# Moving the S5 gate's matrix products behind two more projection tiles in the hand-written order of a hybrid trunk's mixing stage

## The chip, the core and the metric

The kernel runs on one core of one Trainium2 chip. The metric is the device time of one execution in microseconds (us), lower is better. The kernel before takes 1447.62 us in the median of three runs.

## The reference, cut to what matters

The model has two layers. Each layer is a half-step SwiGLU feed-forward block, a mixing block and a second half-step feed-forward block, on 272 tokens (16 learned ones and 256 of the input) of width 1024. The mixing block projects once and feeds four head groups of width 512:

```python
proj = h @ w_in                       # 1024 -> 5136, split into the groups' inputs
y_a = rglru_mixer(a_x, a_gate, ...)   # group A
y_b = gdn_mixer(b_qkv, ...)           # group B: a triangular solve in chunks
y_c = ssd_mixer(c_z, c_xbc, ...)      # group C
y_d = s5_mixer(d_u, ...)              # group D
y = concatenate([y_a, y_b, y_c, y_d]) @ w_out
```

The change is about the end of group D. After its state-space scan has given `y` (512 channels), the S5 mixer does

```python
y = y.reshape(bsz, t, W_GRP) + d_skip * uf
y = jax.nn.gelu(y)
y = y * jax.nn.sigmoid(y @ w_glu.astype(F32))   # the S5 gate: a 512 x 512 product
return rms_norm(y, norm_g)
```

## The kernel before

**Products.** Channels lie on the 128 partitions and tokens along the free dimension. Every large product is made in three passes (`mm3`, lines 229 to 234): the weight and the activation are each split into a rounded part and a remainder, and hi*xh, hi*xl and lo*xh are added up in one PSUM tile. A weight tile is 128 x 1024 (512 KB). It is loaded by SyncE into one of three `raw` buffers (`load`, line 205), split by ScalarE into `hi` (line 215) and by VectorE into `lo` (line 217), four buffers each. `ahead(3)` (line 208) is called behind each tile and keeps three tiles split in advance. The order of the weights is read from the same list of steps that orders the work (`weights`, line 99), so moving a step moves its load and its split with it.

**PSUM.** The products of the weight tiles write into tiles named `g`, from a pool of four; everything smaller writes into `m`, from a second pool of four:

```python
s.pg = pool('pg', 4, bass.MemoryType.PSUM)
s.pm = pool('pm', 4, bass.MemoryType.PSUM)
...
def gps(s):
    return s.pg.tile([P, 512], F32, name=s.nm('g'), tag='g')
```

A `g` tile can be given out again once its last reader is done.

**The mixing stage** walks through `STEPS` (lines 81 to 88), a list written out by hand. A name with a number is one step. The names that this text needs:

- `du`, `k`, `q`, `v`, `cB`, `cC`, `cx`, `cz`, `ax`: one w_in tile each, that is 24 products of 272 (or 256) columns into one `g` tile (`one_tile`, line 323), and behind them the unit that reads this tile. For `q`, `k`, `v`, `cB`, `cC` and `cx` the unit is a four-tap convolution (`conv`, lines 538 to 545: one ScalarE instruction and three VectorE instructions on line 545, all four reading the `g` tile) and a SiLU (lines 551 and 552); for `ax` it is the convolution alone, into `s5b` (line 876; step `ax0` also loads two small weights, line 874); for `cz` the SiLU alone.
- `da0` to `da3`: the skip and the GELU of S5, one quarter of the channels each (lines 1229 and 862 to 865, ScalarE and VectorE in turn). `ds0` to `ds3`: the split of that quarter for `mm3`, into `dU` by ScalarE (line 1236) and `du` by GpSimd (line 1237).
- `dg0`, `dg1`: the S5 gate (`d_glu`, lines 1240 to 1254). Each is one tile of w_glu and fills two `g` tiles with 12 products each, tanh on ScalarE (line 1250) and a gating product on VectorE (line 1252) behind each of the two.
- `dn0`, `dn1`: S5's norm. `bm`, `bf`, `bs`, `bt`, `bo`: the triangular solve of group B (its products are on line 686). `bc`: the chain of small VectorE instructions ahead of that solve (lines 656 to 671), queued behind the last convolution unit before it in the list, `cB1`. `cg`: a product of group C on line 803. `bv2`: transposes on line 628.

```python
def d_glu(s, i):
    ...
    w = s.chunk()
    for m in (2 * i, 2 * i + 1):
        ps = s.gps()
        for k in range(4):
            s.mm3(ps[:, 0:s.N], w, (m % 2) * 4 + k, s.dyh[:, k], s.dyl[:, k], k == 0, k == 3)
```

**The order on each engine** is fixed when the program is built: the tile framework takes the instructions in the order in which the steps issue them as their priority and places them on a modelled timeline, so an instruction that is ready in the model can pass one that is not. Each engine then runs its own list strictly in order on the chip.

Of the kernel before, what the change touches and what calls it, by code (L numbers as in the profile page):

```python
# [80 lines left out]
STEPS_TEXT = '''  # L81
du0 du1 du2 du3 k0 di0 k1 sm k2 do0 tk ks1 R0 ks0 q0 q1 di1 q2 k3 cB0 do1 qs0 qs1 ks3 ks2 q3 di2 qs3 cz0 v0 v1 da0 qs2
do2 v2 be0 di3 bn cC0 bg0 R1 v3 be1 da1 do3 bg1 bg2 cx0 da2 bg3 bv0 da3 cC1 bb bv1 ds0 cB1 bc bm0 cz1 cx1 ds1 cg0 cg1 ds2
ds3 bv2 dg0 ax0 bf00 dg1 bm1 ax1 dn0 bf01 bf02 cx2 bf03 cx3 dn1 ax2 cz2 bf10 bf04 bs00 bf11 bs01 xd0 am2 am1 bs02 ax3
am0 xd1 bs03 am3 bs04 bf12 S0 bf13 ce0 bf14 ag0 bs10 bs11 cz3 bs12 ac ag1 bs13 bs14 bz0 S1 bz1 as0 ag2 xd2 bt0 bz2 ag3
as1 as2 bt1 as3 bz3 bo00 cp0 an0 ce1 S2 bo10 bo30 an1 ce2 bo31 bo01 bo20 cp1 oA0 bo11 bo21 S3 cp2 bo02 cn00 bo32 ce3
bo22 cn01 bo12 cp3 oB0 cn10 cn11 oD0 oC0 oD1 oB1 oA1 oC1
# [1427 lines left out]
```

## Time and profile before

| | before |
|---|---|
| median of three runs | 1447.62 us |
| lowest and highest run | 1442.08 and 1450.54 us |
| the profiled execution's own time | 1442.42 us |
| its span, first to last instruction | 1440.5 us |
| mean granted TensorE clock | 0.969 of 2.4 GHz |
| matmul busy (PE), weight load busy (PEld) | 1392.0 us, 1353.8 us |
| VectorE (DVE), ScalarE (ACT), GpSimd (POOL) busy | 1036.4, 708.4, 205.4 us |

A timeline row gives the start, the duration, the engine, the line, the operation, the output and its inputs by the names of tiles, the shapes, how many equal instructions were merged, and in square brackets the idle time before it with what ended that idle time. `g` and `m` are PSUM tiles, `r` a scratch tile, `xh` and `xl` the split activation.

### The profile page before, as it was taken

Reading aid. Unit: us, or ns where it says so; the run is one execution under the profiler, and the core shown is the slowest. Engines: PE = TensorE matmul, PEld = TensorE weight load, DVE = VectorE, ACT = ScalarE, POOL = GpSimd, SP = SyncE. Lnnn points to the kernel's source line nnn. Section 1 sums busy time; section 2 is a strip of 40 time slices with the busy share of each in tenths; the row PEclk is TensorE's granted clock in tenths of the full one; section 3 lists DMA queues with packets and bytes.
Section 4 is the critical chain, followed back from the end, with each engine's and each line's share of the span. In section 5 each row is a group of like instructions: output and inputs, shape, how many; then the busy total and the mean of one; then the engine's idle time right before and its main releaser. Section 6 shows DMA issues by size and latency. Waiting matters only on the chain. (4 is left out here: it accounts for less than half of the span.)

```text
span 1440.5 us, 27604 instructions
## 1 busy us (share of the span) xinstructions
PE 1392.0 (97%) x10848; PEld 1353.8 (94%) x10848; DVE 1036.4 (72%) x1936; ACT 708.4 (49%) x1226; POOL 205.4 (14%) x235
## 2 busy tenths in 40 slices
PE   7999999998999999999999999999989899999997
PEld 7999998997998999999999999989989889999997
DVE  6998787978985468887656665669888746666653
ACT  6445444454675355554444444444555745544442
POOL 1000010322322320000100000103332223100011
PEclk9999999999997999999999999999999979999998
DMA  7568775654422256777555555556544213666662
GB/s 238 179 188 265 235 254 163 217 171 120 126 77 71 82 155 217 254 230 254 172 162 184 175 170 174 172 161 211 177 127 141 74 45 114 186 187 187 188 182 85
DMA packets 94025, 243.73 MB, mean 169 GB/s; under 512 B 29496, under 2 KB 39496, under 8 KB 93896
## 3 DMA queue, kind: packets, MB, share of 16 engines
q1 hardware_dynamic: 93896, 241.97, 54.2%
q8 instruction: 85, 1.39, 0.4%
q14 instruction: 44, 0.36, 0.1%
HBM read 222.16 MB, written 19.78 MB: 168 GB/s over the span
## 5 line engine op out<-in xcount | busy, mean ns | idle before, releaser
L215 ACT ACTIVATE hi<-raw 128x1024 fp32r<-128x1024 f32 (+1 forms) x382 | 403.3, 1056 | 532.2 <-PE g L233 302.0
L217 DVE TENSOR_TENSOR lo<-raw,hi 128x1024 fp32r<-128x1024 f32 (+1 forms) x382 | 470.2, 1231 | 215.6 <-ACT hi L215 213.9
L232 PE MATMUL g<-xh,hi 128*128 128x272 f32 (+1 forms) x2048 | 597.7, 293 | 12.2 <-ACT hi L215 8.7
L234 PE MATMUL g<-xh,lo 128*128 128x272 f32 (+1 forms) x2048 | 595.8, 292 | 0.8 <-DVE lo L217 0.8
L233 PE MATMUL g<-xl,hi 128*128 128x272 f32 (+1 forms) x2048 | 595.3, 291 | 0.3 <-DVE xl L317 0.3
L232 PEld LDWEIGHTS g<-xh,hi 128*128 128x128 f32 x2048 | 391.4, 191 | 14.7 <-ACT hi L215 8.6
L234 PEld LDWEIGHTS g<-xh,lo 128*128 128x128 f32 x2048 | 390.7, 191 | 2.6 <-DVE lo L217 1.1
L233 PEld LDWEIGHTS g<-xl,hi 128*128 128x128 f32 x2048 | 391.5, 191 | 1.5 <-DVE xl L317 0.6
L277 POOL TENSOR_TENSOR acc<-acc,r 128x272 f32<-128x272 f32 (+1 forms) x42 | 43.3, 1032 | 556.1 <-ACT r L276 555.4
L233 PE MATMUL g<-r,hi 128*128 128x272 f32 (+1 forms) x256 | 73.2, 286 | 0.0
L360 DVE TENSOR_TENSOR r<-r,g 128x272 f32<-128x272 f32 (+1 forms) x88 | 38.1, 432 | 37.5 <-PE g L234 36.0
L545 DVE SCALAR_TENSOR_TENSOR r<-g,small,r 128x269 f32<-128x269 f32 (+2 forms) x120 | 59.1, 493 | 2.0 <-ACT r L542 0.4
L234 PE MATMUL g<-ra,lo 128*128 128x272 f32 (+1 forms) x192 | 55.2, 287 | 0.0
L232 PE MATMUL g<-ra,hi 128*128 128x272 f32 (+1 forms) x192 | 55.1, 287 | 0.0
L233 PE MATMUL g<-rs,hi 128*128 128x272 f32 (+1 forms) x192 | 55.0, 286 | 0.0
L233 PE MATMUL g<-rz,hi 128*128 128x272 f32 (+1 forms) x192 | 55.0, 286 | 0.0
L234 PE MATMUL g<-rq,lo 128*128 128x272 f32 (+1 forms) x192 | 54.6, 287 | 0.0
L232 PE MATMUL g<-rq,hi 128*128 128x272 f32 (+1 forms) x192 | 53.5, 289 | 0.2
L358 DVE TENSOR_TENSOR r<-g,rstd 128x272 f32<-128x272 f32 (+1 forms) x88 | 38.3, 435 | 15.6 <-PE g L234 14.8
L233 PEld LDWEIGHTS g<-r,hi 128*128 128x128 f32 x256 | 48.1, 188 | 0.0
L232 PE MATMUL g<-dU,hi 128*128 128x272 f32 (+1 forms) x96 | 29.7, 309 | 9.8 <-DVE r L545 9.8
L359 ACT ACTIVATE r<-r 128x272 f32<-128x272 f32 (+1 forms) x88 | 36.5, 415 | 5.4 <-DVE r L358 4.2
(412 smaller groups left out, 2461.5 us busy)
## 6 DMA issues: line engine op xcount, KB each, us to landing
raw<-in_wgu_dram SPq DMA_DIRECT2D x176, 512.0 KB
raw<-in_wdn_dram SPq DMA_DIRECT2D x88, 512.0 KB
raw<-in_win_dram SPq DMA_DIRECT2D x80, 512.0 KB
raw<-in_wout_dram SPq DMA_DIRECT2D x32, 512.0 KB
s5a<-spill SPq DMA_DIRECT2D x8, 920.0 KB
s5b<-spill SPq DMA_DIRECT2D x8, 896.0 KB
spill<-s5a SPq DMA_DIRECT2D x8, 648.0 KB
spill<-rx SPq DMA_DIRECT2D x4, 640.0 KB
```

What stands on the lines that cost most here:

```text
L215: nc.scalar.activation(out=hi[:, 0:w], in_=raw[:, 0:w], func=AF.Copy)
L217: ins = nc.vector.tensor_tensor(out=lo[:, 0:w], in0=raw[:, 0:w], in1=hi[:, 0:w].bitcast(F32), op=ALU.subtract)
L232: nc.tensor.matmul(ps, lhsT=hi, rhs=xh, start=start, stop=False)
L233: nc.tensor.matmul(ps, lhsT=hi, rhs=xl, start=False, stop=False)
L234: nc.tensor.matmul(ps, lhsT=lo, rhs=xh, start=False, stop=stop)
L277: (eng or nc.gpsimd).tensor_tensor(out=acc, in0=acc, in1=t, op=ALU.add)
L358: nc.vector.tensor_tensor(out=t, in0=g[:, t0], in1=r, op=ALU.mult)
L359: nc.scalar.activation(out=si, in_=t, func=AF.Silu)
L360: nc.vector.tensor_tensor(out=a, in0=si, in1=u[:, t0], op=ALU.mult)
L545: nc.vector.scalar_tensor_tensor(out=dst[:, o:T], in0=ps[:, 0:T - o], scalar=taps[:, j:j + 1], in1=dst[:, o:T], op0=ALU.mult, op1=ALU.add)
```

## The change

In the list of steps, both steps of the S5 gate and the first step of its norm move back, and the list is otherwise the same. `dg0` stood ahead of `ax0` and now stands behind `ax1`; `dg1` stood between `ax0` and `ax1` and now stands behind `cx2`; `dn0` now stands behind `cx3`.

```diff
-ds3 bv2 dg0 ax0 bf00 dg1 bm1 ax1 dn0 bf01 bf02 cx2 bf03 cx3 dn1 ax2 cz2 bf10 bf04 bs00 bf11 bs01 xd0 am2 am1 bs02 ax3
+ds3 bv2 ax0 bf00 ax1 dg0 bm1 cx2 dg1 bf01 bf02 cx3 dn0 bf03 ax2 dn1 cz2 bf10 bf04 bs00 bf11 bs01 xd0 am2 am1 bs02 ax3
```

The list serves both layers, so the change is made twice.

## Rows read from the trace of the kernel before

**Rows 1.** The page: span, and busy time by engine.
```profile
span 1440.5 us, 27604 instructions
...
PE 1392.0 (97%) x10848; PEld 1353.8 (94%) x10848; DVE 1036.4 (72%) x1936; ACT 708.4 (49%) x1226; POOL 205.4 (14%) x235
```

**Rows 2.** Waits of PE over the whole span: total us, times, longest us.
```profile
PE g L232 <- DVE r L545: 9.8, 2, 6.0
...
PE m L686 <- DVE E L816: 4.9, 1, 4.9
```

**Rows 3.** PE's timeline in the first layer, around the first gate products.
```profile
356.47 0.57 PE L232 MATMUL g<-dU,hi 128*128 128x272 f32 x1 [5.98 <-DVE r L545]
...
360.69 0.39 PE L232 MATMUL g<-dU,hi 128*128 128x272 f32 x1
...
361.55 0.62 PE L803 MATMUL m<-dc 128*128 128x272 f32 x2
...
362.85 0.37 PE L232 MATMUL g<-xh,hi 128*128 128x272 f32 x1
...
365.94 0.29 PE L232 MATMUL g<-dU,hi 128*128 128x272 f32 x1
```

**Rows 4.** PE's timeline in the second layer, the same place.
```profile
1070.63 0.36 PE L232 MATMUL g<-dU,hi 128*128 128x256 f32 x1 [3.87 <-DVE r L545]
...
1074.37 0.28 PE L234 MATMUL g<-dU,lo 128*128 128x256 f32 x1
```

**Rows 5.** One stretch by engine: busy us (instructions) of PE, PEld, DVE, ACT, POOL; granted clock; DMA.
```profile
350.00:360.00 10.00, 4.02 (x19) 3.83 (x19) 6.94 (x16) 5.26 (x12) 3.00 (x4) 0.70 0.41 139
```

**Rows 6.** GpSimd's timeline: the last split of the S5 quarters, both layers.
```profile
355.39 0.76 POOL L1237 TENSOR_TENSOR du<-dp,dU 128x272 fp32r<-128x272 f32 x1 [0.84 <-ACT dU L1236]
...
1069.53 0.72 POOL L1237 TENSOR_TENSOR du<-dp,dU 128x256 fp32r<-128x256 f32 x1 [0.81 <-ACT dU L1236]
```

**Rows 7.** VectorE's timeline in the first layer.
```profile
354.10 0.75 DVE L865 SCALAR_TENSOR_TENSOR dp<-r,r 128x272 f32<-128x272 f32 x1 [0.50 <-ACT r L864]
354.77 1.55 DVE L545 SCALAR_TENSOR_TENSOR r<-g,small,r 128x269 f32<-128x269 f32 x3
356.88 0.44 DVE L552 SCALAR_TENSOR_TENSOR dc<-r,r 128x272 f32<-128x272 f32 x1 [0.56 <-ACT r L551]
357.35 1.57 DVE L545 SCALAR_TENSOR_TENSOR r<-g,small,r 128x269 f32<-128x269 f32 x3
...
359.83 0.16 DVE L656 TENSOR_SCALAR a<-a 68x8 f32<-68x8 f32 x1
...
360.00 0.42 DVE L552 SCALAR_TENSOR_TENSOR rg<-r,g 128x272 f32<-128x272 f32 x1
...
361.54 0.49 DVE L545 SCALAR_TENSOR_TENSOR r<-g,small,r 128x271 f32<-128x271 f32 x1
...
372.25 0.39 DVE L671 COPY a<-a 68x256 f32<-68x256 f32 x1
...
372.90 0.50 DVE L545 SCALAR_TENSOR_TENSOR s5b<-g,small,s5b 128x271 f32<-128x271 f32 x1
```

**Rows 8.** VectorE's timeline in the second layer.
```profile
1068.93 1.55 DVE L545 SCALAR_TENSOR_TENSOR r<-g,small,r 128x269 f32<-128x269 f32 x3
```

**Rows 9.** ScalarE's timeline in the first layer.
```profile
350.41 1.06 ACT L215 ACTIVATE hi<-raw 128x1024 fp32r<-128x1024 f32 x1 [1.50 <-PE g L233]
...
362.90 0.66 ACT L1250 ACTIVATE r<-g 128x272 f32<-128x272 f32 x2
```

**Rows 10.** SyncE's queue in the first layer: the second small load of step ax0.
```profile
337.43 0.38 SPq L874 DMA_DIRECT2D s5b<-in_lw_dram  x1
```

**Rows 11.** VectorE's groups from 359 to 373 us: busy us, mean ns, then idle before.
```profile
L1252 DVE SCALAR_TENSOR_TENSOR dp<-r,dp 128x272 f32<-128x272 f32 x4 | 1.6, 432 | 0.0
...
L545 DVE SCALAR_TENSOR_TENSOR s5b<-g,small,s5b 128x269 f32<-128x269 f32 (+2 forms) x3 | 1.5, 490 | 0.0
```

**Rows 12.** PE's timeline: the longest wait for the solve in each layer.
```profile
428.24 1.13 PE L686 MATMUL m<-rs,rk 128*128 128x128 f32 x8 [1.29 <-DVE rs L722]
...
1143.22 2.05 PE L686 MATMUL m<-rs,rk 128*128 128x128 f32 x8 [4.93 <-DVE E L816]
```

## The prediction

> **What bounds the kernel now.** I read the page first: PE's matmuls are busy for 97% of the span and the weight loads for 94%, no other engine for more than 72% [rows 1]. So time comes from PE's idle stretches and from stretches at its lower clock. Next the waits of PE: the longest that lie inside the mixing stage are two of the same kind, a product of line 232 that waits for a VectorE instruction of line 545, 9.8 us in total [rows 2]. PE's timeline shows where: in both layers it is the first product of step `dg0`, after 5.98 us of idle time in the first layer and 3.87 us in the second [rows 3, 4]. It also shows what follows: behind the wait the products start about 0.23 us apart instead of 0.13, and the granted clock of that stretch is 0.70, a mix of 2.4 and 1.2 GHz [rows 3, 5].
>
> The point on which everything turns is what this wait is for. `dg0` needs two things: its operand, the split S5 quarters, and a free `g` tile.
>
> - The operand. The last quarter's split ends on GpSimd at 355.39 + 0.76 = 356.15 us, and at 1070.25 us in the second layer [rows 6]. The first product reads only the first quarter, which has long been there.
> - The `g` tile. The last tiles of w_in ahead of `dg0` are `cC1`, `cB1`, `cz1` and `cx1`: four tiles, and the pool has four. VectorE reads them in that order: the three taps of `cC1` at 354.77 (its SiLU into `dc` follows), those of `cB1` at 357.35, `cz1`'s SiLU into `rg` at 360.00, the last tap of `cx1` at 361.54 [rows 7]. Until 354.77 + 1.55 = 356.32 us all four are held. PE goes on at 356.47, 0.15 us later. In the second layer the taps end at 1068.93 + 1.55 = 1070.48, and PE goes on at 1070.63, again 0.15 us later [rows 4, 8].
>
> So I take the wait for one on a `g` tile, with the operand coming in 0.17 and 0.23 us sooner: two gates that open at nearly the same time. The profile's own releaser is line 545, which has nothing to do with S5.
>
> By the Trainium skill's page Perfetto Trace Analysis (Identifying Performance Opportunities), bubbles that repeat on an engine that should be full can mean that there is no PSUM for the next tile, and one looks up the semaphore that ends the gap. The trace agrees, with the releaser of line 545 in both layers [rows 2]; by that rule the sum is about 0, by reading the gap as S5's operand coming late it would be -13.3 us, worked out below.
>
> **The change part by part.** No instruction is added or removed; the sum counts where they land.
>
> 1. *The first product behind `cx1`.* With `dg0` moved, the next tile on PE is `ax0`. It needs no S5 operand, but it needs a `g` tile, and the first to come free is still `cC1`'s, at 356.32 us. What frees it, VectorE's queue up to there, belongs to steps that stand ahead of the change in the list, among them the S5 steps `da` whose last instruction at 354.10 is just ahead of the taps [rows 7]. Nothing in it moves. `ax0` starts at about 356.47, and the idle time and the slow products behind it stay. Cost 0. What it would be if the wait went: idle 5.98 + 3.87 us; slow products, 18 starts from 356.47 to 360.69 take 4.22 us where at the pace of the w_in tile behind them (24 in 365.94 - 362.85 = 3.09 us, 0.129 each) they would take 2.32, so 1.90 us; in the second layer 17 starts up to 1074.37 take 3.74 us against 2.19, so 1.55 us. Together 13.3 us [rows 3, 4].
>
> 2. *Weights.* The split into `hi` that ScalarE begins at 350.41 waited for PE to leave a `hi` tile [rows 9]; with four `hi` tiles and the order of the list it is the fourth behind `cx1`, so the three next to be used, now `ax0`, `ax1` and `dg0`, are split by then. The loads change places, all are 512 KB, and PE takes tiles at the same pace: cost 0. On SyncE the two small loads of `ax0` already go out by 337.43 us, 13 us before PE comes to it [rows 10], and they are moved ahead, not back: cost 0.
>
> 3. *The tiles after that.* `ax0` takes what `dg0` took, 356.47 to 361.55; then `cg1` and `bv2` as before until 362.85; `ax1` until 365.94 [rows 3]; `dg0` in two halves until 367.5 and 369.0; `cx2` until 372.1; `dg1` until 375.2; then `cx3`, where it was. For `g` tiles: `ax1` gets `cB1`'s (free at 358.92), `dg0` gets `cz1`'s (360.42) and `cx1`'s (362.03) [rows 7], each before PE asks. `cx2` asks at 369.0. A convolution tile is held long: `ax0`'s third tap ended at 372.90 + 0.50 = 373.40, 7.46 us after its products [rows 3, 7], so it would be free at 361.55 + 7.46 = 369.0; the first half of `dg0` is held only for its tanh, which for both halves was over at 363.56, 2.0 us after `dg0` [rows 3, 9], so at 369.5 at the latest. No margin, but no wait either; `cx3` asks at 375.2 and gets `ax1`'s at 365.94 + 7.46 = 373.4. Cost 0; bounds in the rivals.
>
> 4. *The chain ahead of the solve.* It runs on VectorE from 359.83 to 372.25 and shares it with whatever is ready [rows 7]. Now the taps of `ax0` and `ax1` (0.490 us each, three a tile) come in that stretch and the gate's products (0.432 us, four in all) leave it [rows 11]. That is between 4 x 0.432 = 1.7 us less and 3 x 0.490 = 1.5 us more. It is the same work in another order, so I take 0 and keep about 1.5 us a layer, 3 us in all, on either side.
>
> 5. *The gate itself.* `dg0` ends 369.0 - 361.55 = 7.5 us later and `dg1` 6.2 us (two tiles). `dn0` stays ahead of `xd0`, which takes over the sum's buffer, and S5's part of the output projection stands behind `cn11`, far on. Cost 0, hidden by the tiles in between; if that cover were gone, at most these 6.2 to 7.5 us a layer.
>
> The sum is 0 us. Against its own time the profiled execution stays at 1442.42 us, which is 5.2 us below the median of the three runs and next to the lowest. The forecast is for the median, so 1447.6 us.
>
> **The rivals.** *The operand is the gate after all*, and `ax0` and `ax1` fill the gap: -13.3 us, 1434.3 us. For it: the operand comes only 0.17 us sooner than the tile. Against it: removing that gate leaves the other, and in both layers PE follows the taps by 0.15 us. It needs VectorE to reach `cC1`'s taps 6 us sooner, and VectorE was busy for 6.94 of those 10 us [rows 5].
>
> *The gap goes but is given back.* Later in the stage PE waits for the solve, 1.29 us and 4.93 us [rows 12], and the solve's chain starts on VectorE behind `cB1`, whatever PE has done by then. With half of it back: about -6.7 us, 1440.9 us.
>
> *The `g` tiles run out again*, on the slow side: behind the four long-held tiles now come two more that are held for 7.5 us, before the first gate tile with its short hold. The place is `cx2`, the point is the third tap of `ax0` later than 369.0 us. Priced by the smaller wait of the trace with its slow products, 3.87 + 1.55 = 5.4 us a layer, 10.8 us in all: 1458.4 us. For it: no margin in part 3. Against it: a wait of a full 3.9 us needs the taps that much later than they took before.
>
> **How the numbers follow.** No change 0.70; the operand gate 0.11; given back 0.06; tiles run out again 0.13. Half a per cent, 7.2 us, is about what a measurement of this kernel can tell from no change. Faster by more takes the operand case and a little of the given-back one, 0.14; slower by more takes the last, 0.12, as a short wait falls within; the same gets 0.74. The likeliest case spans the three runs, 1442.08 to 1450.54, widened by the chain's 3 us: 1439 to 1453.5. The range goes somewhat into both other cases, 1437 to 1455 us; left out are the operand case and most of the last, about 0.2.
>
> **What would show it.** Right: in the changed kernel the first product of `ax0`, on `xh`, starts after an idle time of 5 to 6 us in the first layer and about 4 in the second, ended by line 545, 0.15 us behind the first taps into a `dc` tile, with slow products behind it; the gate's first product has no wait. Step 3 is wrong if PE waits for line 545 again between 368 and 376 us; step 4 is wrong if the chain's last copy of line 671 moves by more than 1.5 us. The forecast falls if there is no wait of over 2 us ahead of `ax0`, or if VectorE's order up to `cC1`'s taps is another one.

## The result and the profile after

The kernel after takes 1458.65 us in the median of seven runs (1452.60 to 1465.95), beside 1444.06 us for the kernel before in the same runs. The ratio is 1.011, with a 95% interval of 1.0085 to 1.0135. The change costs about 15 us where the forecast was no change with a range up to 1455 us.

The profiled execution of after took 1465.95 us, the highest of the seven; that of before took 1442.42 us, less than the median. After has the same instructions in the same order up to the place of the change, and it is already about 7.8 us late there. That is spread and not the change: kernels that are equal up to that place reach it anywhere from 356.4 (e2) to 362.9 us (e7). So I compare the stretches below from the end of PE's wait in the first layer on, the one of [rows 3], and leave what lies ahead of it to chance.

The page of after, its span and the busy time by engine; with [rows 1], the same number of products is busy for 10 us more:

```profile
span 1463.4 us, 27601 instructions
...
PE 1401.9 (96%) x10848; PEld 1362.5 (93%) x10848; DVE 1037.2 (71%) x1936; ACT 707.3 (48%) x1226; POOL 203.7 (14%) x235
```

PE's waits in after (total us, times, longest us). With [rows 2]: the wait of line 232 for line 545 is still there, twice. The wait for the solve's line 722, 1.29 us in the first layer of before [rows 12], is 4.3 us:

```profile
PE g L232 <- DVE r L545: 12.6, 2, 6.5
...
PE m L686 <- DVE rs L722: 4.3, 1, 4.3
PE m L686 <- DVE E L816: 3.7, 1, 3.7
```

PE's timeline in after: `ax0`'s first product, the first product of the solve proper (on `rs`), the solve's longest wait, all in the first layer, and `ax0` in the second layer:

```profile
364.29 0.57 PE L232 MATMUL g<-xh,hi 128*128 128x272 f32 x1 [6.05 <-DVE r L545]
...
406.45 1.05 PE L686 MATMUL m<-rs,r 128*128 128x128 f32 x8
...
440.63 1.54 PE L686 MATMUL m<-rs,rk 128*128 128x128 f32 x8 [4.28 <-DVE rs L722]
...
1095.01 0.56 PE L232 MATMUL g<-xh,hi 128*128 128x272 f32 x1 [6.53 <-DVE r L545]
```

The solve's first product in before, in the same view:

```profile
394.85 1.05 PE L686 MATMUL m<-rs,r 128*128 128x128 f32 x8
```

Two things are to be seen. First, the wait that the change might have filled is untouched: `ax0` on `xh` now waits for the same taps, 6.05 us where `dg0` waited 5.98 us [rows 3]. Second, the solve comes later. Its first product is 394.85 - 356.47 = 38.4 us behind the end of that wait in before and 406.45 - 364.29 = 42.2 us in after. In the timeline from [rows 3] on one can also count the tile products (lines 232 to 234) that PE runs ahead of it, from the one that waited: 215 in before and 232 in after. Seventeen more tile products, at the 0.129 us of the prediction 2.2 us, stand ahead of the solve on PE's list, although none of the solve's steps is among those that the diff moves.

### The profile page after: what moved, and what is told of

It reads as the page before. It is cut to its first block, busy times and chain, and to the rows that moved or that the text cites. A ratio compares the mean times of both kernels' runs of the same rounds, so it can differ in the third digit from the quotient of the medians.

```text
span 1463.4 us, 27601 instructions
## 1 busy us (share of the span) xinstructions
PE 1401.9 (96%) x10848; PEld 1362.5 (93%) x10848; DVE 1037.2 (71%) x1936; ACT 707.3 (48%) x1226; POOL 203.7 (14%) x235
## 4 chain that ended last, share of the span: by engine, by line
PE 87%; DVE 5%; DMA 2%; issue 2%; ACT 2%; POOL 1%; SPq 0%; DVEq 0%; POOLq 0%; ACTq 0%
PE g L232 25%; PE g L234 24%; PE g L233 24%; PE m L686 2%; DVE lo L217 1%; PE m L240 1%; PE m L1215 1%; PE m L262 1%; PE m L1179 1%; ACT hi L215 1%; POOL dz L1185 1%; PE m L611 1%; PE m L1213 1%; PE m L826 1%; PE m L1128 0%
## 5 line engine op out<-in xcount | busy, mean ns | idle before, releaser
L302 DVE SCALAR_TENSOR_TENSOR xl<-h,small,xh 128x272 fp32r<-128x272 f32 (+1 forms) x48 | 34.7, 742 | 5.8 <-ACT xh L301 5.8
```

What stands on the lines that cost most here:

```text
L302: nc.vector.scalar_tensor_tensor(out=s.xl[:, k, sl], in0=h, scalar=g[:, k:k + 1], in1=s.xh[:, k, sl].bitcast(F32), op0=ALU.mult, op1=ALU.s ...
```

## The experiments

The theories, in words. *The tail*: the gate's tanh, gating product and square now run on ScalarE and VectorE among the copies of group B's factors (lines 707 and 709) and hold them up. *The lists*: the change makes the framework place the solve's products later on the engines' lists, and that is the loss, whatever caused it. *The second layer*: its lists are reshuffled too. A letter in an expectation has the meaning that the expectation gives it. Steps are changed in the first layer only, unless told otherwise; the second layer then has the old list of steps. In e1, e2 and x1 line numbers are four higher than before, so line 709 is 713 there, 545 is 549, 686 is 690 and 722 is 726. A difference in us behind a ratio is worked out from the ratio, and can be off that of the medians.

**e1 and e2: one layer at a time.**

```diff
-                for name, a in STEPS:
+                for name, a in STEPS_OF[l]:   # e1: new list where l == 0; e2: where l == 1
```

> The new list in the first layer alone; the second layer keeps the old list. Theory A (the gate's late tail stands in the way of group B's solve): the first layer pays what it paid in the changed kernel, measured from the end of the gap ahead of ax0: VectorE's first copy of line 709 comes about 35 us behind line 656's first instruction instead of 32.8 - so at least 2 us later than in the kernel before - and the wait of line 686 for line 722 is 3 us or more instead of 1.3. Total +5 to +9 us, and the second layer runs within 3 us of its old length. Theory B (the changed list only reshuffles everything that the model orders later): the second layer, whose list is old, changes its length by more than 3 us all the same. Theory C (the 7.8 us by which the changed kernel's profile was behind at 350 us is chance): this profile, whose instructions up to there are the same, comes to the gap anywhere between 350 and 359 us.

> The new list in the second layer alone. The first layer is the kernel before, so its gap ahead of dg0 is about 6 us and its solve waits 1.3 us. Theory A: the cost is what the second layer paid in the changed kernel for its own list, +4 to +7 us, and this and the run with the first layer alone add up to the changed kernel's +14.6 us. Theory B: they do not add up; this run alone can be anything from 0 to +15 us.

Measured: e1 1460.41 us, ratio 1.0094 (1.0063 to 1.0125), +13.6 us. e2 1449.4 us, ratio 1.0018 (0.9995 to 1.0041), +2.6 us. Together 16.2 us, beside the 14.6 of the whole and within the uncertainties. Nearly all of it comes of the list in the first layer, where *the tail* had foretold 5 to 9 us; in the second, where it had foretold 4 to 7, the same edit can't be told from nothing. The wait at the changed place is as before in both. PE's timeline of e1 in the first layer, and in the second, which has the old list of steps:

```profile
356.92 0.56 PE L236 MATMUL g<-xh,hi 128*128 128x272 f32 x1 [5.98 <-DVE r L549]
...
1090.39 0.55 PE L236 MATMUL g<-dU,hi 128*128 128x256 f32 x1 [6.82 <-DVE r L549]
```

And that of e2 in the second:

```profile
1070.75 0.36 PE L236 MATMUL g<-xh,hi 128*128 128x272 f32 x1 [3.87 <-DVE r L549]
```

So the wait of the second layer grows from 3.87 to 6.82 us where only the first layer's list was changed, and not at all where the second layer's own was.

**e3: one tile in place of two** behind which each gate step goes.

```diff
-ds3 bv2 dg0 ax0 bf00 dg1 bm1 ax1 dn0 bf01 bf02 cx2 bf03 cx3 dn1 ax2 cz2
+ds3 bv2 ax0 bf00 dg0 bm1 ax1 dg1 bf01 bf02 cx2 dn0 bf03 cx3 dn1 ax2 cz2
```

(in both layers)

> The gate's steps behind one more tile of w_in instead of two (ax0 dg0 ax1 dg1 cx2 dn0). The gap of about 6 and 4 us stays, now ahead of ax0 and ended by line 545. Theory A: the gate's tail falls about 3 us later instead of 6 and meets less of the solve's factors, so the cost is about half: +4 to +9 us. Theory B: no relation to the distance, anything between -5 and +15 us.

Measured: 1461.11 us, ratio 1.010 (1.0066 to 1.0134). Half the move costs as much as the whole, where *the tail* had let me expect about half, so the loss isn't proportional to how late the gate is. The solve's wait is 4.30 us here too, and 234 products stand ahead of its first one.

**e4 and e5: a fifth `g` tile**, with one `m` tile less; e4 with the new list, e5 with the old, both in both layers.

```diff
-s.pg = pool('pg', 4, bass.MemoryType.PSUM)
-s.pm = pool('pm', 4, bass.MemoryType.PSUM)
+s.pg = pool('pg', 5, bass.MemoryType.PSUM)
+s.pm = pool('pm', 3, bass.MemoryType.PSUM)
```

> The changed kernel with five PSUM tiles for g and three for m instead of four and four. If the gap ahead of ax0 is the wait for a g tile, ax0 starts at once and the first gap shrinks from 6 us to under 2 us, or moves by one tile to ax1. If the gap were anything else it stays at 5 us or more ahead of ax0. The total is open, since m has one tile less: 1440 to 1475 us.

> The old list with five PSUM tiles for g and three for m. Both gates of dg0 opened within 0.3 us of each other in the kernel before, so if the operand is the second gate, a fifth g tile alone shortens the gaps ahead of dg0 by no more than about 1 us: first layer 5 us or more. If the g tile had been the only gate, the gap falls to under 3 us as it did ahead of ax0 in the changed kernel with five tiles (2.3 us). Total 1440 to 1455 us, since m with three tiles adds waits of about 2 us a layer.

Measured: e4 1451.21 us, ratio 1.0021 (0.9999 to 1.0044); e5 1452.8 us, ratio 1.0042 (1.0015 to 1.0069). PE's timeline of e4: the first product of `ax0`, and the wait that follows, in the first layer and in the second:

```profile
351.63 0.37 PE L232 MATMUL g<-xh,hi 128*128 128x272 f32 x1
...
358.67 0.57 PE L232 MATMUL g<-xh,hi 128*128 128x272 f32 x1 [2.30 <-DVE r L545]
...
1086.07 0.57 PE L232 MATMUL g<-xh,hi 128*128 128x272 f32 x1 [4.82 <-DVE s5b L545]
```

PE's waits in e5 (total us, times, longest us):

```profile
PE m L686 <- DVE rs L722: 9.5, 2, 5.5
...
PE g L233 <- POOL du L1237: 6.4, 5, 3.8
```

With a tile more, `ax0` has no wait in either layer. The wait has moved one tile on, to the first product of `ax1`, 2.30 and 4.82 us; the expectation of e5 takes the 2.30 us for `ax0`'s. With the old list the gate's first product has no wait either, and its next ones wait for S5's operand (line 1237), 2.6 us together in the first layer and 3.8 us in the second. So the tile was the gate that decided, with the operand close behind it. The time gained is given back: PE waits 9.5 us for the solve in e5, where before has 1.29 and 4.93 [rows 12]. Whether that comes of the order or of the `m` tile that is missing, these runs don't separate. And with five tiles the new list shows no cost against the old one (1.0021 and 1.0042). The same edit of the steps is a loss with one set of lists and none with another, a first sign for *the lists*.

**x0 and x1: no gate tail** in the first layer, with the old list and with the new one.

```diff
-            nc.scalar.activation(out=t, in_=ps[:, 0:s.N], func=AF.Tanh, scale=0.25)
-            nc.vector.scalar_tensor_tensor(out=o, in0=t, scalar=1.0, in1=o, op0=ALU.add, op1=ALU.mult)
-            s.sumsq(s.dacc, o, m == 0)
+            if s.N < T:
+                ...
+            if s.N < T or m == 0:
+                s.sumsq(s.dacc, o, m == 0)
```

> Old list. In the first layer the gate's tail is left out: no tanh, no gating product, and only the first of the four squares, so S5's gate has no effect there. The products stay. This is the baseline for the next run: the first layer shortens by 0 to 3 us against the kernel before.

> The new list in the first layer alone, with the same tail of the gate left out there. Theory A (the tail, late, stands in VectorE's and ScalarE's lists among the factors of group B's solve): without it the first layer costs no more than with the old list and no tail, within 2 us from the end of the gap to the first update of line 726 (36.1 us in the kernel before, 40.8 with the new list). Rival (the taps of ax0, ax1 and cx2, or the order of PE's products, delay the solve): the 4 to 5 us stay.

Measured: x0 1443.21 us, ratio 0.9989 (0.9964 to 1.0013); x1 1449.56 us, ratio 1.0026 (0.9997 to 1.0056). The difference of the medians is 6.3 us where e1 has 13.6. I read this at first as half the loss being the tail's. The ratios' difference, 0.0037 with an uncertainty of about as much, can't carry that: it fits a tail that costs nothing as well as one that costs most of the loss.

The traces speak both ways. By the sign that the expectation names the tail is to blame: the solve's first update (line 726, in x1 730) comes 41.6 us behind the end of the wait in x0 and 42.2 in x1, 0.7 us apart, while e1's comes 4.7 us later than before's. But near the end of the stage the loss is there without a tail. The first product of the output projection on S5's output, in PE's timeline of x0:

```profile
496.89 0.39 PE L232 MATMUL g<-dU,hi 128*128 128x272 f32 x1
```

Of x1:

```profile
504.19 0.29 PE L236 MATMUL g<-dU,hi 128*128 128x272 f32 x1
```

From the end of the wait (359.73 and 357.20 us) that is 137.2 us in x0 and 147.0 in x1, and it is 137.2 in before and 146.6 in e1. So a stage can get as long as e1's with no tail in it. Leaving work out changes the built lists as well, though: 225 products ahead of the solve in x1, between the 215 of x0 and the 232 of e1.

**e6: the contention taken away.** In e1 two VectorE instructions take 1.53 us where they take 0.43 us elsewhere, while GpSimd builds masks (here line 700). VectorE's timeline in e1:

```profile
382.25 1.53 DVE L556 SCALAR_TENSOR_TENSOR cx<-r,r 128x272 f32<-128x272 f32 x1
383.71 1.53 DVE L1256 SCALAR_TENSOR_TENSOR dp<-r,dp 128x272 f32<-128x272 f32 x1
385.17 0.68 DVE L713 COPY rq<-m 128x512 f32<-128x512 f32 x1
```

GpSimd's at the same time:

```profile
382.11 1.37 POOL L700 TENSOR_TENSOR r<-a,cst 128x512 f32<-128x512 f32 x1 [6.48 <-DMA a<-s]
383.45 1.49 POOL L700 TENSOR_TENSOR rk<-a,cst 128x512 f32<-128x512 f32 x1
```

The Trainium skill's page SBUF — State Buffer (Who interferes with whom) says that a VectorE instruction with two inputs in SBUF contends with a GpSimd instruction that reads SBUF, for a pair of ports that only one of them holds at a time. The trace agrees: the VectorE instruction that starts 0.14 us behind GpSimd's takes 1.53 us instead of 0.43. e6 is e1 with these masks issued later on GpSimd, in both layers:

```diff
-        for eng, dst, src in ((nc.vector, m['D'], s.dc), (nc.gpsimd, m['E'], s.dtc16)):
-            eng.tensor_tensor(...)
+        nc.vector.tensor_tensor(out=m['D']...)
+        s.late[b] = lambda: nc.gpsimd.tensor_tensor(out=m['E']...)   # called behind the last factor, after the GpSimd part of dn0
...
```

> The new list in the first layer alone, and in both layers GpSimd's two masks for E are issued behind the norm's two small GpSimd instructions of group D instead of as soon as their input is there. In the run with the new list in the first layer two VectorE instructions just ahead of the first factor's copy took 1.53 us instead of 0.43 while GpSimd made these masks. If that contention is part of the cost, they go back to about 0.43 us and the first copy of line 713 (709 in the kernel before) comes 2 us sooner after the gap, 23 us instead of 24.9 behind line 660 (656); the total falls by 1 to 4 us from 1460.4. If the two were slow for another reason, they stay at 1.5 us.

Measured: 1456.97 us, ratio 1.0089 (1.0059 to 1.0119), beside e1's 1.0094: no gain that can be told from none. VectorE's timeline in e6 shows that the edit did its work (line 709 is 713 here, 1252 is 1259, 686 is 690):

```profile
382.44 0.43 DVE L556 SCALAR_TENSOR_TENSOR cx<-r,r 128x272 f32<-128x272 f32 x1
382.80 0.44 DVE L1259 SCALAR_TENSOR_TENSOR dp<-r,dp 128x272 f32<-128x272 f32 x1
383.15 0.68 DVE L713 COPY rq<-m 128x512 f32<-128x512 f32 x1
...
390.16 0.67 DVE L713 COPY rq<-m 128x512 f32<-128x512 f32 x1
```

PE's timeline in e6 shows that it doesn't matter:

```profile
386.15 1.05 PE L690 MATMUL m<-r,rq 128*128 128x128 f32 x8
...
398.79 1.05 PE L690 MATMUL m<-rs,r 128*128 128x128 f32 x8
...
432.97 2.05 PE L690 MATMUL m<-rs,rk 128*128 128x128 f32 x8 [4.28 <-DVE rs L729]
```

The first copy into `rq` ends at 383.83, and PE runs the product on it at 386.15, with no wait noted: PE is in the middle of a tile that stands ahead of it on its list. The first `rs` product comes 42.1 us behind the end of the wait, as in e1, and the solve's wait is the same 4.28 us. The order on PE is the same as in e1 (232 products), and S5's output product comes 146.5 us behind the end of the wait, in e1 146.6. This is the second sign for *the lists*.

**e7 and e8: one part of the move, and the opposite move.** e7 leaves `dg0` and moves only `dg1` and `dn0`. e8 moves `dg1` ahead of `ax0`, right behind `dg0`. Both leave the second layer's lists nearly as before, which e1 didn't.

```diff
-ds3 bv2 dg0 ax0 bf00 dg1 bm1 ax1 dn0 bf01 bf02 cx2 bf03 cx3 dn1 ax2 cz2
+ds3 bv2 dg0 ax0 bf00 ax1 bm1 cx2 dg1 bf01 bf02 cx3 dn0 bf03 ax2 dn1 cz2
```

```diff
-ds3 bv2 dg0 ax0 bf00 dg1 bm1 ax1 dn0 bf01 bf02 cx2 bf03 cx3 dn1 ax2 cz2
+ds3 bv2 dg0 dg1 ax0 bf00 bm1 ax1 dn0 bf01 bf02 cx2 bf03 cx3 dn1 ax2 cz2
```

> First layer only: dg0 stays where it was, ahead of ax0; dg1 goes behind cx2 and dn0 behind cx3, as in the change. The second layer keeps the old list, and the engines' lists there are nearly those of before. PE's list then holds 233 products of w_in and gate tiles between cx1 and the first product of the solve proper (rs), where before has 215 and the change 232. Theory A (dg1's tail lands among group B's factor copies on ScalarE and VectorE, and PE's list puts the factors behind more tiles for it): the first layer loses 8 to 11 us as with the whole change there, the second layer nothing, ratio about 1.006 to 1.008; the gap at dg0 is 5.98 as before; the solve's wait behind VectorE's rs is above 3 us in the first layer, and 4.9 in the second. Theory B (the cost comes of taking the gate's products away from the gap, so that convolution tiles meet it): within 3 us of before, ratio 0.998 to 1.002. Theory C (the cost is mostly the second layer's lists, reshuffled by the model): also within 3 us.

> First layer only: dg0 and dg1 both ahead of ax0, so the gate's tail comes earlier than before, not later. PE's list has the factors and the solve at the same counts as before (215 products ahead of the first rs product), and the second layer's lists nearly as before. Theory A: no loss, 0 to -3 us against before, ratio 0.998 to 1.001, solve wait 1 to 2 us in the first layer. Theory B (any move of these tiles about the gap costs): +5 us or more. A gain of over 4 us would mean that the gate's tail cost something in before too.

Measured: e7 1451.58 us, ratio 1.0069 (1.0044 to 1.0093), +10.0 us (8.0 between the medians); e8 1444.99 us, ratio 1.0007 (0.9987 to 1.0026). PE's timeline of e7: the first gate product, the first `rs` product, the solve's wait.

```profile
362.91 0.57 PE L232 MATMUL g<-dU,hi 128*128 128x272 f32 x1 [6.07 <-DVE r L545]
...
405.52 1.05 PE L686 MATMUL m<-rs,r 128*128 128x128 f32 x8
...
439.58 1.24 PE L686 MATMUL m<-rs,rk 128*128 128x128 f32 x8 [4.28 <-DVE rs L722]
```

The same three of e8:

```profile
357.72 0.56 PE L232 MATMUL g<-dU,hi 128*128 128x272 f32 x1 [5.99 <-DVE r L545]
...
396.55 1.05 PE L686 MATMUL m<-rs,r 128*128 128x128 f32 x8
...
429.95 1.13 PE L686 MATMUL m<-rs,rk 128*128 128x128 f32 x8 [1.32 <-DVE rs L722]
```

So the tile that comes first behind the wait has no part in it: with `dg0` in its old place the loss is there, 10 us from the first layer alone.

**c0: a swap that has nothing to do with the gate**, to size the reshuffle of the second layer. The instructions come in the order of before up to about 450 us.

```diff
-an1 ce2 bo31 bo01
+an1 bo31 ce2 bo01
```

> First layer only: two steps late in the mixing stage, ce2 and bo31, change places, and the gate stays as before. The first layer is as before up to about 500 us, while the second layer's lists are reshuffled by the model about as much as with the change in the first layer alone. Theory C (the reshuffle costs): the second layer from its S5 step da0 on loses 3 us or more, its gap is longer than 3.87 us, ratio 1.002 or above. Theory A: within 2 us of before, ratio 0.9985 to 1.0015.

Measured: 1446.63 us, ratio 1.0025 (1.0000 to 1.0050), +3.6 us (3.0 between the medians), at the edge of its uncertainty. The wait in the second layer grows from 3.87 [rows 4] to 4.66 us, PE's timeline:

```profile
1077.46 0.55 PE L232 MATMUL g<-dU,hi 128*128 128x256 f32 x1 [4.66 <-DVE r L545]
```

An edit of two steps in the first layer reaches the second, since the model places everything behind it anew. What that costs is not clear of noise here. With e7's 10.0 us the 3.6 make e1's 13.6, but c0's lists aren't e1's, so this share is likely and not shown; in e1 itself the wait at the head of the second layer's stage is 2.95 us longer and its solve wait 2.37 us instead of 4.93.

**e9 and e10: the solve moved on the lists, the gate untouched.** e9 takes the tile of `ax3` ahead of the second batch's factors; e10 takes `xd0` and `am2` ahead, so that the later half of the solve stands behind fewer tiles.

```diff
-cz2 bf10 bf04 bs00 bf11 bs01 xd0 am2 am1 bs02 ax3
+cz2 ax3 bf10 bf04 bs00 bf11 bs01 xd0 am2 am1 bs02
```

```diff
-cz2 bf10 bf04 bs00 bf11 bs01 xd0 am2 am1 bs02 ax3
+cz2 xd0 bf10 bf04 am2 bs00 bf11 bs01 am1 bs02 ax3
```

> First layer only, and the gate is not touched: the tile of ax3 moves ahead of bf10, so that PE's list places group B's solve behind more tiles. Between cx1 and the first rs product stand 234 products of tiles (before 215, the change 232), and at the longest wait of the solve 360 as in both. Theory A' (what the change costs in the first layer is the place of the solve in PE's list, whatever put it there): 5 to 11 us slower, ratio 1.0035 to 1.008, first rs product about 41 to 42.5 us behind the end of the gap where before has 38.4, a solve wait of 3 us or more where before has 1.29. Theory D (the cost is the gate's tail running among the factor copies on ScalarE and VectorE): the gate's tail is where it was, so within 3 us of before and a solve wait of 1 to 2 us.

> First layer only, and the gate is not touched: xd0 goes ahead of bf10, and am2 ahead of bs00. PE's list then has the later half of the solve at fewer products: 232, 248, 267, 308 and 314 where before has 233, 250, 274, 334 and 334, and its longest wait at 357 (before 360). Theory A': the solve ends sooner against the tiles, 0 to 5 us faster, ratio 0.9965 to 1.0. Theory D says nothing of it: 1.000. If it is slower, fewer products ahead of the solve are worth nothing, since the chain of the solve's own copies on VectorE then ends last.

Measured: e9 1442.39 us, ratio 0.9985 (0.9958 to 1.0012); e10 1446.78 us, ratio 1.0015 (0.9992 to 1.0039). e9 is a miss for the theory in the form in which it was put. PE's timeline of e9, with the place of [rows 3] first:

```profile
360.75 0.56 PE L232 MATMUL g<-dU,hi 128*128 128x272 f32 x1 [5.97 <-DVE r L545]
...
402.14 1.05 PE L686 MATMUL m<-rs,r 128*128 128x128 f32 x8
...
433.19 1.13 PE L686 MATMUL m<-rs,rk 128*128 128x128 f32 x8 [1.41 <-ACT r L551]
```

The first `rs` product is late as foreseen, by 402.14 - 360.75 = 41.4 us, behind 234 products. But the solve catches up, and its wait is 1.41 us. A late start alone is no loss. What after, e1, e3, e6 and e7 share is the wait of 4.28 to 4.30 us further on. Ahead of it PE has only 17 tile products between the solve's product on `rz,rn` and the next one on `rs,rk`, to cover VectorE's work in between; before has 26, e9 20 and e10 43 (0.11 us of wait on `rs,rk` there). e10 is a miss too: it has covered the remaining 1.29 us and gains nothing that can be measured.

**e11: the gate exactly where the change puts it, another order behind it.** If the tail is to blame, the loss must stay.

```diff
-ds3 bv2 dg0 ax0 bf00 dg1 bm1 ax1 dn0 bf01 bf02 cx2 bf03 cx3 dn1 ax2 cz2 bf10 bf04 bs00 bf11 bs01 xd0
+ds3 bv2 ax0 bf00 ax1 dg0 cx2 dg1 bf01 bf02 cx3 dn0 bf03 ax2 dn1 cz2 bf04 bs00 bm1 bf10 bf11 bs01 xd0
```

> First layer only: the gate's steps stand exactly where the change puts them (dg0 behind ax1, dg1 behind cx2, dn0 behind cx3), but other steps behind them change places: bm1, bf10 and bf11 go behind bf04 and bs00. PE's list then has the first rs product at 222 (before 215, change 232), the later half at 284 and 320 where the change has 295 and 343, and between the rz,rn product and the rs product that waits 31 tile products instead of 17 (before 26). The second layer's lists are those of before. Theory A'' (the loss in the first layer is the solve coming too late in the engines' lists, with too few products left to cover it): the solve's wait falls from 4.28 to 1.5 us or less, PE's last w_in product comes 84 to 86 us behind the end of the gap (before 83.5, change 89.5), the whole 0 to 5 us slower than before, ratio 0.999 to 1.0035. Theory D (the cost is the gate's tail where it is, among the factor copies): the tail is as late as in the change, so the loss of the first layer stays, 8 to 11 us, ratio 1.0055 to 1.0075, and the solve's wait is above 3 us.

Measured: 1445.54 us, ratio 1.0013 (0.9992 to 1.0034). PE's timeline of e11:

```profile
359.11 0.56 PE L232 MATMUL g<-xh,hi 128*128 128x272 f32 x1 [6.05 <-DVE r L545]
...
399.00 1.05 PE L686 MATMUL m<-rs,r 128*128 128x128 f32 x8
...
431.52 1.13 PE L686 MATMUL m<-rs,rk 128*128 128x128 f32 x8 [1.36 <-DVE E L816]
```

The solve's first product comes 39.9 us behind the end of the wait, behind 222 products, with 31 to cover the later wait, which is 1.36 us. The gate is as late as in the change all the same. The tanh of `dg1`, on ScalarE's timeline of e11:

```profile
383.70 0.38 ACT L1250 ACTIVATE r<-g 128x272 f32<-128x272 f32 x1
...
386.92 0.38 ACT L1250 ACTIVATE r<-g 128x272 f32<-128x272 f32 x1
```

Of e1:

```profile
381.63 0.38 ACT L1254 ACTIVATE r<-g 128x272 f32<-128x272 f32 x1
...
385.61 0.38 ACT L1254 ACTIVATE r<-g 128x272 f32<-128x272 f32 x1
```

That is 24.6 and 27.8 us behind the end of the wait in e11, 24.7 and 28.7 in e1, and among the copies of the factors in both; before has 11.2 and 14.1. The loss of the first layer is gone with the tail this late, so its lateness alone isn't the loss. One rival stays untested: e11's order of the other steps was not run with the gate in its old place, so it might gain by itself what the gate costs. Against it, e11 is within 1.5 us of before at every place that the table times, and nowhere ahead of it.

The kernels side by side, first layer, counted and read in each PE timeline; times in us from the end of the wait of [rows 3]. "Cover" is the number of tile products between the `rz,rn` and the `rs,rk` product, "last tile" the start of the last of the 432 products of w_in and gate tiles, "idle" PE's idle time up to it, and "S5 out" the first product of the output projection on S5's output:

| kernel | products ahead of the solve | first rs product | cover | wait on rs,rk | last tile | idle | S5 out | ratio |
|---|---|---|---|---|---|---|---|---|
| before | 215 | 38.4 | 26 | 1.29 | 83.5 | 1.3 | 137.2 | |
| e8 | 215 | 38.8 | 26 | 1.32 | 83.9 | 1.4 | 139.9 | 1.0007 |
| e10 | 211 | 39.7 | 43 | 0.11 | 83.6 | 0.7 | 140.2 | 1.0015 |
| e11 | 222 | 39.9 | 31 | 1.36 | 84.2 | 1.4 | 137.9 | 1.0013 |
| e9 | 234 | 41.4 | 20 | 1.41 | 86.7 | 2.4 | 133.4 | 0.9985 |
| e6 | 232 | 42.1 | 17 | 4.28 | 89.4 | 5.5 | 146.5 | 1.0089 |
| e1 | 232 | 42.2 | 17 | 4.28 | 89.5 | 5.0 | 146.6 | 1.0094 |
| e7 | 233 | 42.6 | 17 | 4.28 | 89.9 | 5.3 | 147.3 | 1.0069 |
| after (both layers) | 232 | 42.2 | 17 | 4.28 | 89.6 | 5.0 | 146.7 | 1.011 |
| x0 (no tail) | 215 | 40.5 | 26 | 1.32 | 85.6 | 2.4 | 137.2 | 0.9989 |
| x1 (no tail) | 225 | 40.4 | 25 | 2.31 | 89.0 | 3.3 | 147.0 | 1.0026 |

Up to S5's output product the losing kernels are 9.3 to 10.2 us behind before. The long wait goes with that loss in four of them, but x1 is as late with a wait of 2.31 us, and e9's last tile is 3.2 us late with no loss at the end. So the runs point to the order, and not to the work that was moved; which trait of the order makes the loss, they don't show.

## Why the prediction was wrong

**Step 1 was right**, and by its own test: `ax0`'s first product on `xh`, which needs no S5 operand, waits 6.05 us for line 545, and with a fifth `g` tile it has no wait (e4). The slow products stay too: 18 starts in 4.21 us, as before. In the second layer after has 6.53 us where about 4 was said, but e2, whose first layer is as before, has 3.87 there, and e1, with the old list of steps there, 6.82; the rest comes from the reshuffled lists. One reading was off, without a part in the sum: the 4.93 us for the solve [rows 12] are a longer wait inside the stage than the second layer's 3.87. **Steps 2 and 3 were right** too: PE has no second wait for line 545 at `cx2` or `cx3` (e1 has one of 0.59 us on the tile behind them), nor one for a weight that before lacked. The rival of `g` tiles that run out named 1458.4 us, next to what was measured, and it is nevertheless wrong: its wait isn't there.

**Step 4** held by its own test and missed the point. The chain's last copy on line 671 comes 12.7 us behind its first instruction in e1, as against 12.4 in before [rows 7]. But the chain from there to the solve, factors included, was given only its VectorE work of 1.5 us a layer as a bound.

**Step 5 is the step that failed**: "Cost 0, hidden by the tiles in between; if that cover were gone, at most these 6.2 to 7.5 us a layer." It asked who needs the gate's output, and nobody does for a long time. It took for granted that the other steps keep their places on the engines' lists. They don't: the lists are built from a model of the whole, in which the moved steps take the engines at other times. Even the gate came otherwise than said: PE makes `dg1`'s products 6.1 us later, near the 6.2 of step 5, but its two tanh stand further back on ScalarE's list and run 13.5 and 14.6 us later (e1 against before). PE's list got the next two factor products behind 180 and 189 tile products where both stood behind 175, the solve behind 232 where it was 215, and the later `rs,rk` product with 17 to cover it where it had 26. On the chip PE keeps to its list, also where the operand of a later product is there already (e6).

What this measured in the first layer, e1 against before: up to the last tile 89.5 - 83.5 = 6.0 us, of which 5.0 - 1.3 = 3.7 is idle time, 3.0 of it the longer wait of [rows 12]. The remaining 2.3 us are products that ran slower: PE has the same 632 to start in this stretch in both, at a granted clock of 0.97 in before and 0.96 in e1. Behind the last tile PE has no large product for some 19 us in either kernel, and from there to S5's output product e1 takes 57.1 us and before 53.7, another 3.4 us, at a lower granted clock. The window from 460 to 480 us of before (busy us and instructions of PE, PEld, DVE, ACT, POOL; granted clock; DMA):

```profile
460.00:480.00 20.00, 20.00 (x128) 17.88 (x126) 8.81 (x28) 8.14 (x20) 9.52 (x12) 0.75 0.13 35
```

Of after, the stretch as far behind the wait's end:

```profile
467.80:487.80 20.00, 19.67 (x99) 17.19 (x99) 6.83 (x20) 8.62 (x25) 6.84 (x8) 0.64 0.00 1
```

Of e1:

```profile
460.00:480.00 20.00, 19.68 (x87) 16.76 (x86) 5.76 (x19) 7.68 (x25) 6.38 (x7) 0.56 0.00 1
```

This last part can't be put down to the change: e8 and e10, which show no loss, take 56.0 and 56.6 us from the last tile on, e11 53.7 and e9 46.7. The whole: about 10 us of the first layer (e7, and 9.5 in e1's and after's own traces), about 3.6 us of reshuffled lists in the second (c0, likely), and 2.6 us that e2 can't tell from nothing.

What stays open: why the second layer is spared with the same edit (e2), beyond that its solve wait is 5.0 us there with either list; how the framework's model comes to its places; and which trait of the order costs the first layer its 9.5 us, beyond the 3.0 us of the longer wait. No version beat both kernels by more than the noise; e8 and e11 equal the kernel before.

## What to carry to other kernels

Where lists are built from a model, a step that is moved moves what isn't named in the diff: before costing a move at zero, compare the built order of every engine, and count how much work stands ahead of the chain that ends last and how much covers its longest wait. A loss that appears all at once, doesn't grow with the size of the move (e3) and vanishes when other steps change places (e11) points to the order and not to the work that was moved. A price that comes out right isn't a mechanism that is right: look for the wait itself.

## What the runs showed that I had not expected

Equal kernels spread widely: the kernel before alone ran from 1436.11 to 1450.29 us in the 25 runs beside e7, e8 and c0, and from 1436.08 to 1456.13 in the 29 beside e5, e6, x0 and x1, so that one profile of each (1442.42 and 1465.95 us) overstates the difference of the medians (23.5 us for 14.6), and a stretch compared by their absolute times was 7.8 us off before the change had begun. A wait that is taken away at the head of a stage was given back at the solve (e5: the gap shorter, 9.5 us of waits for line 722). And a VectorE contention of 2 us that stands on the way to the solve was worth nothing (e6), because the product that needed the result was placed later anyway.
